# Gated linear attention in a one-core trunk: k's two parts stacked on the array's rows, v's two parts copied to the other half by DMA

## The chip, the cores and the metric

The kernel runs on one core of a Trainium2 chip. The metric is device time in microseconds (us) of one execution; the kernel before takes 2559.77 us, the median of 3 runs (2559.71 to 2559.84).

## What is computed

A trunk of two layers over 16 learned meta tokens and 1024 frames, width 1024. Layer 0 mixes with chunked gated linear attention (GLA), layer 1 with a sparse attention that the change doesn't touch; a SwiGLU follows each. Of the GLA, for each of 4 heads and each chunk of 64 positions:

```
cum = jnp.cumsum(gi, axis=2)
tot = cum[:, :, -1:, :]
S = jnp.exp(tot[:, :, 0, :, None]) * S + jnp.einsum(
    'bhcd,bhce->bhde', ki.astype(jnp.float32) * jnp.exp(tot - cum), vi.astype(jnp.float32))
o = jnp.einsum('bhcd,bhde->bhce', qi.astype(jnp.float32), S)
```

The state S of a head is 128 x 256 (key width by value width). A chunk adds k^T v to it, a product that contracts over 64 positions. Before it, S is scaled by the chunk's decay.

## The kernel before

Every fp32 operand of a product is split in two parts that TensorE takes in its fp32r type: a high part, which ScalarE casts, and a low part, which VectorE gets as the value less the high part (`split`, L224). A product is then the sum of three: high by high, high by low, low by high (`mm3`, L228).

The GLA stage goes through the four heads. For a head it projects q (in three stretches of tokens, L590), the output gate r (in six, L603), and then v, one tile of tokens at a time (`proj_tm`, L243): tile 0 holds the 16 meta tokens, tiles 1 to 8 hold 128 positions each, so two chunks: rows 0 to 63 and rows 64 to 127. After the projection of a tile, `core` (L513) splits v out of PSUM (`vh`, `vl`) and the decayed k out of SBUF (`kh`, `kl`), and puts three later steps on a list:

- `state` (L534), two ticks later: the products k^T v of the tile's two chunks, three each, into two PSUM tiles `us`; then VectorE adds them to the scaled state `sf` (L548), and the state is split into `sh` and `sl`.
- `read` (L554), four ticks later: q by the states of both chunks, 128 x 512 (L559), then the mean square on ScalarE (L564), its root, and the scaling on VectorE (L568).
- `gated` (L571), six ticks later: two transposes on TensorE (L575) and the gating on VectorE (L580).

`later.tick()` (L614) runs what is due after each tile, so on TensorE the order of a full tile's work is: projection of tile i, transposes of tile i-3, read of tile i-2, state of tile i-1, projection of tile i+1. A scheduler then sets the order within each of the other engines; each engine runs its own instructions in that order, and one that waits holds all behind it.

The two chunks of a tile lie on different rows of the array, and the six products alternate between them:

```
for step, (a, b) in enumerate([(kh, vh), (kh, vl), (kl, vh)]):
    for c, (r0, r1) in enumerate(halves):
        nc.tensor.matmul(us[c], a[r0:r1, :], b[r0:r1, :], start=step == 0, stop=step == 2)
```

GpSimd (POOL in the profile) issues few transfers in this stage, all of them from `rel_table` (L618), which head 1 calls for the layer after: four small writes of a bias table to DRAM (`s_rel`, L637), then eight transfers that write it out 128 times, shifted, per attention head (`s_skew`, L644, DRAM to DRAM). They go through the software DMA queue q0. Weights come by SyncE through q1.

Of the kernel before, what the change touches and what calls it, by code (L numbers as in the profile page):

```python
# [9 lines left out]
F32 = mybir.dt.float32  # L10
F32R = mybir.dt.float32r
# [99 lines left out]
class Trunk:  # L111
# [244 lines left out]
    def gla(self):  # L356
        nc, tc, io, w, later = self.nc, self.tc, self.io, self.w, self.later
        v = nc.vector
        with ExitStack() as ctx:
            g = ctx.enter_context(tc.tile_pool(name="gla", bufs=1))  # L360
            s2 = ctx.enter_context(tc.tile_pool(name="gla2", bufs=2))
            s3 = ctx.enter_context(tc.tile_pool(name="gla3", bufs=3))
            kt = g.tile([128, 9, 512], F32, name="kt")
# [124 lines left out]
            ats, step = {}, 0  # L488
# [3 lines left out]
            for tiles, j, i in order:  # L492
                if step in norms:
                    c, d = norms[step]
# [18 lines left out]
            def core(h, i, p, qh, ql, prev):  # L513
                rows = TT[i][1]
                two = i > 0
                hs = slice(h * 128, h * 128 + 128)
                vh = s3.tile([128, 256], F32R, name="vh")
                vl = s3.tile([128, 256], F32R, name="vl")
                kh = s3.tile([128, 128], F32R, name="kh")
                kl = s3.tile([128, 128], F32R, name="kl")  # L520
                if i == 0:
                    val = s3.tile([128, 256], F32, name="on")[:META, :]
                    self.meta(val, p[:, :256])
                else:
                    val = p[:, :256]
                self.split(vh[:rows, :], vl[:rows, :], val)
                self.split(kh[:rows, :], kl[:rows, :], kt[:rows, i, hs])
                st = {}
                sf = s2.tile([128, 512], F32, name="sf")
                sh = s2.tile([128, 512], F32R, name="sh")  # L530
# [1 line left out]
                cols = 512 if two else 256  # L532

                def state():  # L534
                    halves = [(0, 64), (64, 128)] if two else [(0, rows)]
                    us = [self.ps()[:, :256] for _ in halves]
                    for step, (a, b) in enumerate([(kh, vh), (kh, vl), (kl, vh)]):
                        for c, (r0, r1) in enumerate(halves):
                            nc.tensor.matmul(us[c], a[r0:r1, :], b[r0:r1, :], start=step == 0,
                                             stop=step == 2)  # L540
                    before = prev.get("s")
                    for c in range(len(halves)):
                        o = sf[:, c * 256 : c * 256 + 256]
                        uc = us[c]
                        if before is None:
                            v.tensor_copy(o, uc)
                        else:
                            v.scalar_tensor_tensor(o, before, dec[:, i, h, c : c + 1], uc,  # L548
                                                   op0=OP.mult, op1=OP.add)
                        before = o  # L550
                    prev["s"] = before
                    self.split(sh[:, :cols], sl[:, :cols], sf[:, :cols])
# [18 lines left out]
                def gated():  # L571
# [5 lines left out]
                    for j in range(2):  # L577
# [3 lines left out]
                                               self.gains[:, 5, k : k + 1], r, op0=OP.mult, op1=OP.mult)  # L581

                later.at(2, state)
                later.at(4, read)
                later.at(6, gated)
# [995 lines left out]
```

## Time and profile before

| | |
|---|---|
| median of 3 runs | 2559.77 us (2559.71 to 2559.84) |
| profiled execution, its own time | 2560.66 us |
| its span, first to last instruction | 2558.9 us |
| TensorE busy (PE) | 2506.4 us, 98% |
| VectorE (DVE), ScalarE (ACT), GpSimd (POOL) busy | 51%, 36%, 14% |
| mean granted clock of TensorE | 0.992 of full |
| products with k and v of `state` (L539) | 68 groups, from 142.2 to 405.0 us of the span |

The profile is one execution. Its rows give the start and the length of each instruction by engine, what it waited for, and for a DMA the time from issue to landing. A product's length in the rows holds its way through the array, so lengths of successive products overlap; what a product costs is the distance from its start to the next one's. "Granted clock" is the share of TensorE's full clock that the chip let through.

### The profile page before, as it was taken

Reading aid. Unit: us, or ns where it says so; the run is one execution under the profiler, and the core shown is the slowest. Engines: PE = TensorE matmul, PEld = TensorE weight load, DVE = VectorE, ACT = ScalarE, POOL = GpSimd, SP = SyncE. Lnnn points to the kernel's source line nnn. Section 1 sums busy time; section 2 is a strip of 40 time slices with the busy share of each in tenths; the row PEclk is TensorE's granted clock in tenths of the full one; section 3 lists DMA queues with packets and bytes.
Section 4 is the critical chain, followed back from the end, with each engine's and each line's share of the span. In section 5 each row is a group of like instructions: output and inputs, shape, how many; then the busy total and the mean of one; then the engine's idle time right before and its main releaser. Section 6 shows DMA issues by size and latency. Waiting matters only on the chain. (4 is left out here: it accounts for less than half of the span.)

```text
span 2558.9 us, 37579 instructions
## 1 busy us (share of the span) xinstructions
PE 2506.4 (98%) x15098; PEld 2325.8 (91%) x15098; DVE 1310.1 (51%) x2798; ACT 917.9 (36%) x1890; POOL 354.7 (14%) x461
## 2 busy tenths in 40 slices
PE   7999999999999999999999989999999999999997
PEld 6999999999999999999878979999988888888887
DVE  7575566643334433344769697753633333333336
ACT  5764453521111111111668567752511111111115
POOL 3000000111111111110202254521100000000001
PEclk9999999999999999999999999999999999999999
DMA  3113013123333333332321111131111111111111
GB/s 121 42 33 112 26 50 101 50 87 119 111 112 115 112 117 108 114 116 71 119 100 50 67 34 34 67 116 67 62 38 50 50 50 50 50 50 41 43 50 66
DMA packets 68786, 189.97 MB, mean 74 GB/s; under 512 B 7066, under 2 KB 18610, under 8 KB 65795
## 3 DMA queue, kind: packets, MB, share of 16 engines
q1 hardware_dynamic: 62642, 154.31, 18.0%
q0 software_dynamic: 5968, 33.26, 3.8%
q8 instruction: 118, 1.93, 0.3%
q14 instruction: 58, 0.47, 0.1%
HBM read 150.74 MB, written 41.58 MB: 75 GB/s over the span
## 5 line engine op out<-in xcount | busy, mean ns | idle before, releaser
L230 PE MATMUL ps<-xh,wh 128*128 128x344 f32 (+5 forms) x2808 | 946.9, 337 | 1.7 <-DVE qf L1039 1.3
L231 PE MATMUL ps<-xl,wh 128*128 128x344 f32 (+5 forms) x2808 | 943.0, 336 | 1.6 <-POOL xl L226 1.0
L232 PE MATMUL ps<-xh,wl 128*128 128x344 f32 (+5 forms) x2808 | 941.9, 335 | 1.9 <-DVE wl L197 1.9
L230 PEld LDWEIGHTS ps<-xh,wh 128*128 128x128 f32 x2808 | 529.2, 188 | 32.3 <-DVE qf L1039 1.6
L231 PEld LDWEIGHTS ps<-xl,wh 128*128 128x128 f32 x2808 | 529.6, 189 | 31.1 <-POOL xl L226 1.5
L232 PEld LDWEIGHTS ps<-xh,wl 128*128 128x128 f32 x2808 | 529.9, 189 | 29.0 <-DVE wl L197 2.5
L715 DVE TENSOR_TENSOR t<-sg,ps 128x344 f32<-128x344 f32 (+4 forms) x116 | 65.1, 561 | 639.3 <-PE ps L232 637.6
L192 ACT CAST wh<-wraw 128x1056 fp32r<-128x1056 f32 (+2 forms) x160 | 163.9, 1049 | 583.0 <-PE ps L231 576.2
L728 DVE TENSOR_TENSOR h<-h,ps 128x344 f32<-128x344 f32 (+3 forms) x456 | 251.4, 567 | 164.4 <-PE ps L232 164.3
L230 PE MATMUL ps<-hh,wh 128*128 128x512 f32 (+2 forms) x800 | 280.5, 351 | 0.0
L231 PE MATMUL ps<-hl,wh 128*128 128x512 f32 (+2 forms) x800 | 280.3, 350 | 0.0
L232 PE MATMUL ps<-hh,wl 128*128 128x512 f32 (+2 forms) x800 | 280.0, 350 | 0.0
L197 DVE TENSOR_TENSOR wl<-wraw,wh 128x1056 fp32r<-128x1056 f32 (+2 forms) x158 | 191.8, 1236 | 74.1 <-ACT wh L192 71.9
L230 PE MATMUL ps<-wh,xh 128*128 128x256 f32 (+9 forms) x560 | 171.9, 307 | 7.2 <-ACT xh L225 4.6
L232 PE MATMUL ps<-wh,xl 128*128 128x256 f32 (+9 forms) x560 | 167.3, 299 | 5.0 <-DVE xl L226 3.0
L714 ACT ACTIVATE sg<-ps 128x344 f32<-128x344 f32 (+4 forms) x116 | 57.7, 498 | 301.2 <-PE ps L232 301.1
L231 PE MATMUL ps<-wl,xh 128*128 128x256 f32 (+9 forms) x560 | 165.7, 296 | 0.0
L230 PEld LDWEIGHTS ps<-hh,wh 128*128 128x128 f32 x800 | 150.2, 188 | 14.6
L231 PEld LDWEIGHTS ps<-hl,wh 128*128 128x128 f32 x800 | 150.4, 188 | 14.3
L232 PEld LDWEIGHTS ps<-hh,wl 128*128 128x128 f32 x800 | 150.7, 188 | 13.8
L225 ACT CAST hh<-t 128x344 fp32r<-128x344 f32 (+4 forms) x116 | 60.1, 518 | 285.7 <-DVE t L715 285.7
L230 PEld LDWEIGHTS ps<-wh,xh 128*128 128x128 f32 x560 | 109.0, 195 | 13.2 <-ACT xh L225 4.9
(304 smaller groups left out, 3252.4 us busy)
## 6 DMA issues: line engine op xcount, KB each, us to landing
wraw<-in_w_fi SPq DMA_DIRECT2D x44, 528.0 KB, 3.9
wraw<-in_w_fi SPq DMA_DIRECT2D x44, 496.0 KB, 5.0
wraw<-in_w_fo SPq DMA_DIRECT2D x22, 528.0 KB, 3.9
wraw<-in_w_fo SPq DMA_DIRECT2D x22, 496.0 KB, 5.2
s_skew<-s_rel POOLq DMA_DIRECT2D x8, 583.5 KB, 14.2
h<-in_ht SPq DMA_DIRECT2D x8, 520.0 KB, 4.6
wraw<-s_skew SPq DMA_DIRECT2D x8, 520.0 KB, 3.5
sg<-in_w_dq SPq DMA_DIRECT2D x16, 256.0 KB, 4.2
```

The lines of the kernel that those rows point to most:

```text
L192: nc.scalar.copy(hi[:, a:e], r[:, : e - a])
L197: self.wlow.tensor_sub(lo[:, c:d], r[:, c - a : d - a], hi[:, c:d].bitcast(F32))
L225: self.nc.scalar.copy(hi, src)
L230: mm(p, sh, mh, start=first, stop=False, skip_group_check=True)
L231: mm(p, sh, ml, start=False, stop=False, skip_group_check=True)
L232: mm(p, sl, mh, start=False, stop=last, skip_group_check=True)
L714: nc.scalar.activation(sg[:, :n], pg[:, :n], AF.Silu)
L715: v.tensor_mul(t[:, :n], sg[:, :n], pu[:, :n])
L728: v.tensor_add(self.h[:, d, a : a + n], self.h[:, d, a : a + n], p[:, :n])
```

## The change

The three products of a chunk become two, over all 128 rows. `ks[:, c, :]` holds k's high part of chunk c on the chunk's own 64 rows and its low part on the other 64. `vs[:, c, :]` holds v's high part (columns 0 to 255) and low part (256 to 511) on both halves: they are computed on the chunk's own rows, and a transfer within SBUF, issued by GpSimd, copies them to the other rows. A product over 128 rows then sums (high k + low k) by high v, and a second one (high k + low k) by low v; low by low, left out before, is in it. The splits of v and k are made per chunk, so on 64 rows. Tile 0 keeps three products on its 16 rows. `ks` has three buffers, `vs` two.

```diff
-                vh = s3.tile([128, 256], F32R, name="vh")
-                vl = s3.tile([128, 256], F32R, name="vl")
-                kh = s3.tile([128, 128], F32R, name="kh")
-                kl = s3.tile([128, 128], F32R, name="kl")
+                ks = s3.tile([128, 2, 128], F32R, name="ks")
+                vs = s3.tile([128, 2, 512], F32R, name="vs", bufs=2)
...
-                self.split(vh[:rows, :], vl[:rows, :], val)
-                self.split(kh[:rows, :], kl[:rows, :], kt[:rows, i, hs])
+                if two:
+                    for c, (r, o) in enumerate(((0, 64), (64, 0))):
+                        own, src = vs[r : r + 64, c, :], slice(r, r + 64)
+                        self.split(own[:, :256], own[:, 256:], val[src, :])
+                        nc.gpsimd.dma_start(vs[o : o + 64, c, :], own)
+                        hi, ksrc = ks[r : r + 64, c, :], kt[src, i, hs]
+                        nc.scalar.copy(hi, ksrc)
+                        v.tensor_sub(ks[o : o + 64, c, :], ksrc, hi.bitcast(F32))
+                else:
+                    self.split(vs[:rows, 0, :256], vs[:rows, 0, 256:], val)
+                    self.split(ks[:rows, 0, :], ks[:rows, 1, :], kt[:rows, i, hs])
...
-                    halves = [(0, 64), (64, 128)] if two else [(0, rows)]
-                    us = [self.ps()[:, :256] for _ in halves]
-                    for step, (a, b) in enumerate([(kh, vh), (kh, vl), (kl, vh)]):
-                        for c, (r0, r1) in enumerate(halves):
-                            nc.tensor.matmul(us[c], a[r0:r1, :], b[r0:r1, :], start=step == 0,
-                                             stop=step == 2)
+                    us = [self.ps()[:, :256] for _ in range(2 if two else 1)]
+                    mm = nc.tensor.matmul
+                    for c, u in enumerate(us):
+                        if two:
+
+                            mm(u, ks[:, c, :], vs[:, c, :256], start=True, stop=False)
+                            mm(u, ks[:, c, :], vs[:, c, 256:], start=False, stop=True)
+                            continue
+                        mm(u, ks[:rows, 0, :], vs[:rows, 0, :256], start=True, stop=False)
+                        mm(u, ks[:rows, 0, :], vs[:rows, 0, 256:], start=False, stop=False)
+                        mm(u, ks[:rows, 1, :], vs[:rows, 0, :256], start=False, stop=True)
```

The instructions on TensorE, VectorE, ScalarE and GpSimd differ in the GLA stage alone; behind it the order is the same, but for line numbers (L539 becomes L549 and L550, L548 becomes L562, L564 becomes L578, L568 becomes L582, L580 becomes L594, L637 and L644 become L651 and L658).

TensorE, a full tile of head 0, from the end of `read` to the next projection. Before (`vh`, `vl`, `kh`, `kl` are the parts of v and k; x2 is one for each chunk):

```order
L231 MATMUL ps<-sl,qh 128x512
L232 MATMUL ps<-sh,ql 128x512
L539 MATMUL ps<-vh,kh 128x256 x2
L539 MATMUL ps<-vl,kh 128x256 x2
L539 MATMUL ps<-vh,kl 128x256 x2
L230 MATMUL ps<-wh,xh 128x256
```

And now:

```order
L231 MATMUL ps<-sl,qh 128x512
L232 MATMUL ps<-sh,ql 128x512
L549 MATMUL ps<-vs,ks 128x256
L550 MATMUL ps<-vs,ks 128x256
L549 MATMUL ps<-vs,ks 128x256
L550 MATMUL ps<-vs,ks 128x256
L230 MATMUL ps<-wh,xh 128x256
```

Six products on 64 rows became four on 128; their place between `read` and the next projection is the same.

ScalarE at the same place of head 0, now: the casts of v's two chunks in tile 5 (`vs_1633`), the squares of `read` (L578, `on_1657`) between them, with the engines that each waits for.

```order
L225 CAST vs_1633<-ps_1607 64x256 [waits DMASW5_49,DMASW6_49,PE_49,Activation_49]
L578 ACTIVATE on_1657,ss_1656<-ps_1652 64x256 [waits PE_49]
L578 ACTIVATE on_1657,ss_1656<-ps_1652 64x256
L225 CAST vs_1633<-ps_1607 64x256 [waits DVE_49]
L532 CAST ks_1778<-kt_92 64x128 [waits PE_49]
```

Before, one cast of 128 rows stood ahead of both squares; now the second chunk's cast stands behind them, and it waits for VectorE.

GpSimd around head 1, before: the small writes of the bias table, then the eight long ones, then the work of the next stage.

```order
L637 DMA s_rel<-rt_2288 8x396
L637 DMA s_rel<-rt_2293 8x396
L637 DMA s_rel<-rt_2298 8x264
L637 DMA s_rel<-rt_2339 8x111
L644 DMA s_skew<-s_rel 128x1167 x8
L226 TENSOR_TENSOR xl_68<-no_5341,xh_67 128x352
```

And now, with what each waits for (DMASW are the semaphores of transfers that GpSimd issued earlier; `vs_2339` is tile 1 of head 1, `vs_2391` tile 2, `vs_2449` tile 3):

```order
L651 DMA s_rel<-rt_2355 8x111 [waits Activation_49]
L530 DMA vs_2339<-vs_2339 64x512 [waits DMASW5_49,DMASW7_49,DMASW0_49,DVE_49]
L530 DMA vs_2339<-vs_2339 64x512 [waits DMASW6_49,DVE_49]
L658 DMA s_skew<-s_rel 128x1167 [waits DMASW3_49,DMASW4_49,DMASW2_49,DMASW1_49]
L530 DMA vs_2391<-vs_2391 64x512 [waits DVE_49] x2
L658 DMA s_skew<-s_rel 128x1167 x3
L658 DMA s_skew<-s_rel 128x1167 [waits DMASW5_49]
L658 DMA s_skew<-s_rel 128x1167 [waits DMASW6_49]
L658 DMA s_skew<-s_rel 128x1167 [waits DMASW7_49]
L658 DMA s_skew<-s_rel 128x1167 [waits DMASW0_49]
L530 DMA vs_2449<-vs_2449 64x512 [waits DMASW1_49,DVE_49]
L530 DMA vs_2449<-vs_2449 64x512 [waits DMASW2_49,DVE_49]
```

One `s_skew` transfer stands between the copies of tiles 1 and 2, and seven between those of tiles 2 and 3; behind them the copies of tiles 3 to 8 and of heads 2 and 3 follow on the same queue. Head 0 has its 16 copies ahead of `s_rel`.

## Rows read from the trace of the kernel before

**Rows 1.** The page: busy time, share of the span and instructions of each engine

```profile
PE 2506.4 (98%) x15098; PEld 2325.8 (91%) x15098; DVE 1310.1 (51%) x2798; ACT 917.9 (36%) x1890; POOL 354.7 (14%) x461
```

**Rows 2.** Busy time by stretch: stretch, length, PE, PEld, DVE, ACT, POOL, PEclk, DMA, GB/s

```profile
158.62:163.13 4.51, 4.51 (x37) 3.96 (x37) 4.12 (x16) 2.45 (x8) 0.00 (x0) 1.00 0.00 0
```

**Rows 3.** Timeline of TensorE, a tile of head 0: start, length (us), line, operation

```profile
157.53 0.38 PE L575 MATMUL ps<-ident,on 128*128 128x128 f32 x2
157.66 0.48 PE L230 MATMUL ps<-sh,qh 128*128 128x512 f32 x1
157.98 0.40 PE L231 MATMUL ps<-sl,qh 128*128 128x512 f32 x1
158.21 0.40 PE L232 MATMUL ps<-sh,ql 128*128 128x512 f32 x1
158.54 0.39 PE L539 MATMUL ps<-vh,kh 64*128 64x256 f32 x2
158.76 0.28 PE L539 MATMUL ps<-vl,kh 64*128 64x256 f32 x2
158.88 0.28 PE L539 MATMUL ps<-vh,kl 64*128 64x256 f32 x2
159.09 0.39 PE L230 MATMUL ps<-wh,xh 128*128 128x256 f32 x1
...
162.02 0.38 PE L575 MATMUL ps<-ident,on 128*128 128x128 f32 x2
```

**Rows 4.** Groups by line and shape, 139 to 410 us: busy us, mean ns

```profile
L226 DVE TENSOR_TENSOR vl<-ps,vh 128x256 fp32r<-128x256 f32 x32 | 13.5, 422 | 13.0 <-ACT vh L225 12.4
L225 ACT CAST vh<-ps 128x256 fp32r<-128x256 f32 x32 | 11.9, 372 | 26.6 <-PE ps L232 26.4
L226 DVE TENSOR_TENSOR kl<-kt,kh 128x128 fp32r<-128x128 f32 x30 | 8.6, 286 | 1.9 <-ACT kh L225 1.6 <-PE ps L232 0.2
```

**Rows 5.** Timeline of VectorE, head 0: small steps of the root, then with a split between

```profile
160.87 0.16 DVE L267 TENSOR_TENSOR rs<-rs 128x1 f32<-128x1 f32 x1
161.06 0.16 DVE L268 TENSOR_TENSOR rs<-rs 128x1 f32<-128x1 f32 x1
...
176.32 0.15 DVE L268 TENSOR_TENSOR rs<-rs 128x1 f32<-128x1 f32 x1
176.39 0.29 DVE L226 TENSOR_TENSOR kl<-kt,kh 128x128 fp32r<-128x128 f32 x1
```

**Rows 6.** DMA issues: transfer, queue, count, KB each, us from issue to landing

```profile
wraw<-in_onehot SPq DMA_DIRECT2D x1, 132.0 KB, 2.3
s_rel<-rt POOLq DMA_DIRECT2D x1, 3.5 KB, 2.8
wh<-s_dq_h POOLq DMA_DIRECT2D x4, 1024.0 KB, 5.2
```

**Rows 7.** Timeline of ScalarE, head 0: tile 1, and the tile of rows 3

```profile
143.31 0.41 ACT L225 CAST sh<-sf 128x256 fp32r<-128x256 f32 x1 [0.28 <-DVE sf L546]
...
159.52 0.20 ACT L564 ACTIVATION_READ_ACCUMULATOR on<-ps 64x1 f32 x1
```

**Rows 8.** Timeline of TensorE, head 0: tile 1's first state product

```profile
145.78 0.39 PE L539 MATMUL ps<-vh,kh 64*128 64x256 f32 x2
```

**Rows 9.** Timeline of GpSimd, head 1: the eight long transfers' issues

```profile
222.34 4.10 POOL L644 DMA_DIRECT2D s_skew<-s_rel  x8 [2.79 <-DMA s_rel<-rt]
```

**Rows 10.** `s_skew` alone: from issue to landing, the first transfer, then the eighth

```profile
DMA to landing us min/median/max: 7.6/7.6/7.6
...
DMA to landing us min/median/max: 17.5/17.5/17.5
```

**Rows 11.** Busy time by stretch: the long transfers (DMA share, GB/s at the end)

```profile
224.00:242.00 18.00, 18.00 (x145) 16.11 (x144) 14.93 (x54) 10.62 (x32) 2.44 (x5) 1.00 0.95 260
```

**Rows 12.** Timeline of TensorE, head 1: tile 3's first state product

```profile
229.79 0.39 PE L539 MATMUL ps<-vh,kh 64*128 64x256 f32 x2
```

**Rows 13.** Busy time by stretch: TensorE at a lower granted clock

```profile
68.00:74.00 6.00, 5.84 (x23) 4.82 (x24) 6.00 (x11) 3.78 (x11) 2.91 (x3) 0.51 0.00 0
```

More of the change, by code (lines that the diff above doesn't have):

```diff
@@ L534, in state @@
                 def state():
-                    halves = [(0, 64), (64, 128)] if two else [(0, rows)]
-                    us = [self.ps()[:, :256] for _ in halves]
-                    for step, (a, b) in enumerate([(kh, vh), (kh, vl), (kl, vh)]):
-                        for c, (r0, r1) in enumerate(halves):
-                            nc.tensor.matmul(us[c], a[r0:r1, :], b[r0:r1, :], start=step == 0,
-                                             stop=step == 2)
+                    us = [self.ps()[:, :256] for _ in range(2 if two else 1)]
[8 more added lines that the diff above has]
+                        mm(u, ks[:rows, 1, :], vs[:rows, 0, :256], start=False, stop=True)
                     before = prev.get("s")
-                    for c in range(len(halves)):
+                    for c in range(len(us)):
                         o = sf[:, c * 256 : c * 256 + 256]
```

## The prediction

> **What bounds the kernel now.** I read the page's busy shares first: TensorE is busy 98% of the span [rows 1], so what is saved on it is saved in the end, and what makes it wait is lost. Then the stretch of one tile of head 0, because an average over the kernel says nothing about this stage: there TensorE has no gap, VectorE is busy 4.12 of 4.51 us [rows 2]. So the stage has one full engine and one nearly full. Then TensorE's timeline of that tile [rows 3]: from one pair of transposes (157.53) to the next (162.02) is 4.49 us, the price of a tile.
>
> **The products.** In rows 3 the six products stand as three pairs, each pair with one start: the two chunks run side by side on their halves of the array. The price is read from distances between starts. A 256-column product in a row of its kind costs 0.12 (158.76 to 158.88). The last read product, 512 columns, costs 0.23 when its like follows (157.98 to 158.21) but 0.33 before the pairs; the first pair costs 0.22 and the last 0.21. So the group costs 0.10 ahead of it + 0.22 + 0.12 + 0.21 = 0.65 us: three slots of 0.12 and about 0.1 of extra at each change of shape. The change puts four products of the common shape there: 4 x 0.12 = 0.48. It saves 0.17 us a tile, 32 tiles, **5.4 us**, and nothing else on TensorE. The tile costs 4.32. The Trainium skill, TensorEngine Tiling (Array Packing), Tiling Modes, speaks against the change: tiles of 64 rows work independently and in parallel. By that alone three slots become four, and the sum would be 32 x 0.12 = 3.8 us slower; the same section says that a change of mode drains the array, and the three extra gaps in rows 3 agree with it.
>
> **The splits.** Each split of v and k is now made twice on half the rows. The length goes by columns, so I take the same price for 64 rows: per tile VectorE gets 0.42 + 0.29 more, ScalarE 0.37 and a cast of k, no longer [rows 4]. ScalarE has room (2.45 of 4.51 [rows 2]). VectorE has not; but in its new order the small steps of the root alternate with the splits of k and the update of the state, where before they stood in a chain. In a chain such a step comes 0.19 us after the last; ahead of a split that doesn't need it it costs 0.07 [rows 5], and of some five such places each gives 0.12 back. I take 0.1 us of the 0.71 as left, VectorE's tile at about 4.6 us beside the 4.49 of now, hidden by the waits below, and price the rest as a rival.
>
> **The wait for v's copy.** This is new: `state` now waits for a chain of casts, subtractions, GpSimd's issue and a transfer. The trace has no transfer within SBUF. The nearest rows for the time from issue to landing: 2.3 us for 132 KB issued by SyncE, 2.8 for a small one by GpSimd, 5.2 for 1 MB by GpSimd [rows 6]. The copy has 128 KB; I take **2.8**, the row of its own queue, and keep 2.3 and 3.3 for the range (5.2 is eight times the bytes).
> - *A full tile, head 0.* I count from the end of its projection (157.53). The second chunk's cast stands behind the squares of `read`, which end at 159.72 [rows 7], so at +2.2; cast 0.37, subtraction 0.42 and handing over put the issue at +3.15 and the landing at +5.95. TensorE wants it one tile (4.32) and transposes, read and the first chunk's products (0.13 + 0.78 + 0.24) later, at +5.47. It waits 0.48. That delay gives the next tile's copy as much room, so about every other wait falls away: 0.24 a tile, for tiles 3 to 7 together 1.2 us. Queued behind TensorE's wait is everything it does; behind GpSimd's only further copies.
> - *Tile 1 of a head.* There is no read yet, so TensorE comes early: 145.78 [rows 8], and 0.24 later for the second chunk. The second cast stands behind that of `sh`, which ends at 143.72 [rows 7]; with 0.37, 0.42 and handing over behind a subtraction of `sl`, the issue comes at 144.75 and the landing at 147.55. Wanted at 146.0: a wait of 1.5.
> So a head waits 2.7 us; heads 0, 2 and 3 **8.1 us**.
>
> **The long transfers in head 1.** This is the term that decides. GpSimd issues eight `s_skew` transfers from 222.34 to 226.44, 0.51 each [rows 9]. The first landed 7.6 us after its issue, at 229.9; the eighth, issued at 225.9, after 17.5, at 243.4; six others between in the order of issue [rows 10]. From 224 to 242 the 16 DMA engines were 95% busy at 260 GB/s [rows 11]. In the new order all eight stand ahead of the copies of tile 3 on GpSimd, seven of them behind tile 2's, in the same DMA queue, and the copies wait in addition for semaphores that the earlier transfers use. If the queue is served in order, tile 3's copy lands when the eighth has landed: 243.4, plus 1.0 for the two copies of tile 2 that now lie between (256 KB at 260 GB/s), plus about 0.5 of its own, so at about 245. TensorE's products of that tile started at 229.79 [rows 12] and can't be passed. That is **15.2 us** of delay up to there, with the waits of tiles 1 and 2 of this head and the two tiles' saving in it. For tiles 4 to 7 I add 1.0. TensorE stands idle for some 10 us of it (and some 4 at tile 2, whose copy stands behind the first long transfer). Where it idled before, the granted clock fell: from 68 to 74 us it was 0.51, the lower of the two levels, 1.2 GHz [rows 13], which costs half of 6 us. I take **2 us**, between 0 (it falls and rises within the idle time) and 3.5.
>
> **The sum.** -5.4 + 0.3 (two tiles' saving, counted in the 15.2) + 8.1 + 15.2 + 1.0 + 2.0 = +21.2 us. The profiled execution took 2560.66 with a span of 2558.9; the median of 3 is 0.9 below it, and the difference counts on either. Forecast: 2559.8 + 21.2 = **2581 us**. Its own range: a copy that lands after 2.3 or 3.3 us shifts every later wait by up to 0.25 a tile and tile 1's by 0.5, about 1.5 us a head, -6 or +6 in all; the clock -2 or +1.5: 2573 to 2589.
>
> **The rivals.**
> 1. *The copies pass the long transfers.* If the queue shares its engines among transfers, tile 3's copy needs only to be issued: the first long transfer landed at 229.9 [rows 10], and the second chunk's copy waits for a semaphore that the second one uses, free some 2.5 us later; it lands near 235.5. Head 1 loses about 5.5 in place of 15.2, and no clock: -5.1 + 8.1 + 5.5 + 1.0 = +9.5, 2569 us. For it: the first long one took 7.6 us, more than an eighth of the 21 that all took. Against: they landed one by one in order of issue.
> 2. *VectorE becomes the bound.* If the alternation hides nothing, a full tile needs 4.49 + 0.71 = 5.2 us on VectorE, 0.88 above TensorE's 4.32; five tiles of four heads give 17.6 in place of 4.6 us of waits there (3 x 1.2 + 1.0), 13 more: 2594 us. For it: how full VectorE is [rows 2]; against: [rows 5]. It decides from about 4.6 us a tile on.
> 3. *GpSimd's issue is held up.* If an issue had to wait for VectorE's instruction to end, up to the longest of its stage, some 0.7 us, each copy lands that much later: at most 0.35 a tile and 0.7 for tile 1, so 8 to 9 us over four heads, 2590 us. Against: the eight issues took 4.10 us, 0.51 each, and VectorE was busy 14.93 of 18 us there [rows 9, 11]. The Trainium skill, SBUF — State Buffer, SBUF: two separate sides, has the rule: a DMA from GpSimd can't have its descriptors written while VectorE runs in certain two-port modes; those 0.51 us show no such stall.
> 4. *Not slower: the copies land in time.* If a copy lands within about 2.0 us and those of head 1 are let through at once, only tile 1's wait stays, some 0.7 a head, and the saving stays: -5.4 + 2.8 = -2.6, 2557 us; with no waits at all 2554.4. It decides at a landing of 2.3 us for the full tiles (5.95 less 5.47 below 2.8), and for head 1 at a queue that lets small transfers by. Against: 2.8 for the small one of GpSimd [rows 6].
> 5. *The count of products.* By the lengths of 0.28 in rows 3, one product fewer in each of 64 chunks would save 18 us; the pairs with one start exclude it.
>
> **How the numbers follow.** Forecast 0.62, copies pass 0.18, VectorE 0.09, held-up issue 0.05, not slower 0.05, others 0.01. A change of 0.2% is 5.1 us, about what a measurement of this kernel can tell from none. Below 2554.7 lies only the end of the fourth rival: faster 0.03. Within 0.2% lie the rest of it and the low end of the first: same 0.06. Slower 0.91. The range takes in the forecast's own 2573 to 2589, nearly all of the first rival (2569, 4 either way), the third and the lower part of the second: 2565 to 2592.
>
> **What would show it.** Right: in head 1 a gap of about 10 us on TensorE ahead of tile 3's state products, ended by the DMA of `vs`, with the landing of the last `s_skew` just before it; a lower clock for some us after it; in heads 0, 2 and 3 a gap of 1 to 2 us ahead of tile 1's and some of 0.3 to 0.8 later; products of 0.12 us, four to a tile. Wrong: a small gap in head 1 (rival 1), VectorE without idle time and TensorE waiting for `sl` or for PSUM (rival 2), issues of the copies longer than 0.5 us (rival 3), no gaps at all (rival 4).

## The result and the profile after

The changed kernel takes 2587.84 us, the median of 4 runs (2587.49 to 2588.48); the kernel before, in the same session, 2559.81 (2559.71 to 2560.50). The ratio is 1.0109, with an interval of 1.0097 to 1.0120: 28.0 us slower. The forecast was 2581 us with a range of 2565 to 2592, so the sign and the range hold, and the time lies 6.8 us above the forecast.

Two lines of the page of the changed kernel, the busy times and one of the DMA issues (transfer, queue, count, KB each, median us from issue to landing):

```profile
PE 2508.5 (97%) x15034; PEld 2332.1 (90%) x15034; DVE 1336.7 (52%) x2862; ACT 939.6 (36%) x1954; POOL 387.5 (15%) x525
...
vs<-vs POOLq DMA_DIRECT2D x64, 128.0 KB, 2.2
```

Against [rows 1] TensorE's busy time hardly moved while the span grew by 26.8 us (2585.7 in place of 2558.9): the loss is idle time. And the copy within SBUF, which no row of before could price, lands after 2.2 us in the median, a little under the forecast's 2.8.

TensorE's timeline of the changed kernel, in head 0 (start and length in us; in brackets the idle time before and what ended it):

```profile
146.84 0.36 PE L549 MATMUL ps<-vs,ks 128*128 128x256 f32 x1 [0.67 <-DMA vs<-vs]
...
154.95 0.35 PE L549 MATMUL ps<-vs,ks 128*128 128x256 f32 x1 [0.16 <-DMA vs<-vs]
...
159.00 0.28 PE L549 MATMUL ps<-vs,ks 128*128 128x256 f32 x1
159.11 0.28 PE L550 MATMUL ps<-vs,ks 128*128 128x256 f32 x1
159.23 0.28 PE L549 MATMUL ps<-vs,ks 128*128 128x256 f32 x1
159.35 0.28 PE L550 MATMUL ps<-vs,ks 128*128 128x256 f32 x1
159.47 0.28 PE L230 MATMUL ps<-wh,xh 128*128 128x256 f32 x1
...
164.51 0.35 PE L549 MATMUL ps<-vs,ks 128*128 128x256 f32 x1 [0.74 <-DMA vs<-vs]
...
169.36 0.36 PE L549 MATMUL ps<-vs,ks 128*128 128x256 f32 x1 [0.39 <-DVE rs L270]
```

Four products cost 0.47 us (159.00 to 159.47), and without a wait they are as good as the forecast had them [rows 3]. But each head has a handful of waits for v's copies, most of them for the second chunk's. A releaser like `rs` at the end is the latest event by the profile; the product itself needs `vs` and `ks`.

The same timeline in head 1, at tile 3:

```profile
246.45 0.55 PE L549 MATMUL ps<-vs,ks 128*128 128x256 f32 x1 [12.06 <-DMA vs<-vs]
246.80 0.41 PE L550 MATMUL ps<-vs,ks 128*128 128x256 f32 x1
```

The products that ran at 229.79 before [rows 12] now run at 246.45, behind 12.06 us of idle time. Why so late is told by the transfers' own rows, which answer to [rows 9, 10]: the last two `s_skew`, then a copy of tile 3 and the last one issued behind it (issue, and time to landing):

```profile
L658 POOL DMA_DIRECT2D s_skew<-s_rel x2: 515/515/515, 230.0 to 230.5; - x2
DMA to landing us min/median/max: 15.0/15.3/15.5
...
L530 POOL DMA_DIRECT2D vs<-vs x1: 541/541/541, 231.0 to 231.0; - x1
DMA to landing us min/median/max: 15.3/15.3/15.3
...
L530 POOL DMA_DIRECT2D vs<-vs x1: 509/509/509, 239.5 to 239.5; - x1
DMA to landing us min/median/max: 7.8/7.8/7.8
```

The eighth `s_skew` lands at about 246.0 (230.5 + 15.5), the copy issued behind it at 246.3, one issued at 239.5 at 247.3. They land one by one in the order of their issue.

Busy time by stretch of the changed kernel (columns as in [rows 2]): the idle time, the 4.6 us behind it, the next 5, and three tiles of head 0:

```profile
240.00:244.00 4.00, 0.00 (x0) 0.00 (x0) 0.00 (x0) 0.00 (x0) 0.00 (x0) 0.50 1.06 323
246.40:251.00 4.60, 4.55 (x21) 4.58 (x22) 2.23 (x5) 1.21 (x3) 0.00 (x0) 0.50 0.01 2
251.00:256.00 5.00, 5.00 (x41) 4.86 (x40) 2.93 (x10) 3.03 (x10) 1.02 (x2) 0.98 0.18 37
...
162.30:176.70 14.40, 12.32 (x85) 10.87 (x84) 13.62 (x46) 9.09 (x26) 2.93 (x6) 1.00 0.30 61
```

After the idle time TensorE ran 4.6 us at a granted clock of 0.50, the lower level, with 21 products where 41 go into the next 5 us: about 2 us lost. And in the three tiles of head 0 VectorE is busy 13.62 of 14.40 us, more than TensorE, and between 157 and 176 us it has no gap above 0.04 us: a sign that a second thing is wrong in this stage.

It shows in VectorE's own timeline: the starts of one and the same instruction of four successive tiles, the scaling by the root.

```profile
159.26 0.98 DVE L582 TENSOR_SCALAR on<-ps,rs 64x256 f32<-64x256 f32 x2
...
164.38 0.98 DVE L582 TENSOR_SCALAR on<-ps,rs 64x256 f32<-64x256 f32 x2
...
169.26 0.98 DVE L582 TENSOR_SCALAR on<-ps,rs 64x256 f32<-64x256 f32 x2
...
174.62 0.97 DVE L582 TENSOR_SCALAR on<-ps,rs 64x256 f32<-64x256 f32 x2
```

(174.62 - 159.26) / 3 = 5.12 us a tile, where TensorE's work, in a tile without a wait, is 4.24 and the forecast had 4.6 for VectorE.

The copies go out later for it. In the tile whose projection ends at 158.08 the first chunk's cast on ScalarE is done at 158.70, and VectorE comes to the subtraction 1.57 us later, behind steps of the root and the scaling of another tile:

```profile
158.33 0.37 ACT L225 CAST vs<-ps 64x256 fp32r<-64x256 f32 x1 [0.34 <-PE ps L232]
...
160.27 0.42 DVE L226 TENSOR_TENSOR vs<-ps,vs 64x256 fp32r<-64x256 f32 x1
```

The second chunk's cast waits for that subtraction, and its copy is issued at 162.17.

To see which head pays, the table gives for each kernel below the time from the first state product of a head's tile 0 to that of the next head, and for head 3 to its last state product, all read from TensorE's timeline of the profiled execution. Among head 3's last state products TensorE already does products of the next stage, at 0.16 us each, and not equally many: 48 stand ahead of the last state product before, 51 in the change, 58 in the change without copies, 64 with all remedies. So this column counts work that is no loss. The column behind it runs on to the first product that reads `hh`, in the next stage, by which every kernel has done the same work there; it is the one to compare. The last column is the median of the runs. Medians of the kernel before in these sessions lay between 2559.78 and 2560.63, its single runs between 2557.8 and 2561.2, so differences of 1 us between rows of that column mean nothing.

| kernel | head 0 | head 1 | head 2 | head 3, last state | head 3 to `hh` | median, us |
|---|---|---|---|---|---|---|
| before | 75.76 | 73.44 | 73.38 | 40.32 | 200.40 | 2559.8 |
| the change | 78.82 | 90.80 | 76.49 | 44.44 | 203.78 | 2587.8 |
| copies by SyncE | 78.05 | 87.59 | 76.47 | 44.01 | 203.35 | 2583.7 |
| change without copies | 75.12 | 72.81 | 72.81 | 43.12 | 201.47 | 2561.7 |
| before, split by halves | 75.73 | 73.44 | 73.39 | 44.01 | 203.33 | 2563.5 |
| products alone | 73.63 | 71.26 | 71.24 | 38.89 | 198.84 | 2552.0 |
| early table | 79.21 | 76.38 | 76.48 | 44.55 | 203.89 | 2574.1 |
| early table, k low on GpSimd | 78.40 | 75.58 | 75.52 | 46.01 | 204.99 | 2572.2 |
| the same, state later | 79.57 | 74.63 | 74.64 | 43.21 | 202.95 | 2570.2 |
| no copies, k low on GpSimd | 73.67 | 73.16 | 71.39 | 42.77 | 200.95 | 2556.6 |
| early table, casts first | 79.66 | 76.33 | 76.33 | 45.00 | 204.22 | 2572.4 |
| all remedies | 74.10 | 72.16 | 72.15 | 44.93 | 202.94 | 2559.5 |
| all remedies in heads 0 to 2 | 74.52 | 71.52 | 71.35 | 40.30 | 200.36 | 2554.9 |
| before, early table | 76.17 | 73.46 | 73.39 | 40.47 | 200.44 | 2560.7 |

The four heads with the column to `hh` make 422.98 us before and 449.89 in the change: of the 28.0 us by the medians the profiled executions show 26.9 in this stage.

### The profile page after: what moved, and what is told of

It is laid out like the page before. It is cut to its first block, busy times and chain, and to the rows that moved or that the text cites. A ratio compares the mean times of both kernels' runs of the same rounds, so it can differ in the third digit from the quotient of the medians.

```text
span 2585.7 us, 37811 instructions
## 1 busy us (share of the span) xinstructions
PE 2508.5 (97%) x15034; PEld 2332.1 (90%) x15034; DVE 1336.7 (52%) x2862; ACT 939.6 (36%) x1954; POOL 387.5 (15%) x525
## 5 line engine op out<-in xcount | busy, mean ns | idle before, releaser
L231 PEld LDWEIGHTS ps<-hl,wh 128*128 128x128 f32 x800 | 150.3, 188 | 14.3
L232 PEld LDWEIGHTS ps<-hh,wl 128*128 128x128 f32 x800 | 150.5, 188 | 13.9
```

Of the source, the lines that this page charges most:

```text
L231: mm(p, sh, ml, start=False, stop=False, skip_group_check=True)
L232: mm(p, sl, mh, start=False, stop=last, skip_group_check=True)
```

## The experiments

**1. Copies by SyncE.** Is it the queue that makes head 1's copies late, or the full DMA engines?

```
-                        nc.gpsimd.dma_start(vs[o : o + 64, c, :], own)
+                        nc.sync.dma_start(vs[o : o + 64, c, :].bitcast(F32), own.bitcast(F32))
```

> The change with v's copies issued by SyncE on its own queue in place of GpSimd's. Theory (the copies of tile 3 of head 1 stand in order behind the eight s_skew transfers in one queue): they now pass, the idle time of 12.06 us ahead of tile 3's state products goes, and head 1 costs what head 0 and head 2 cost (3.1 us in place of 17.4): 2587.8 - 14.3 = 2573.5 us. Rival (the copies are late because the 16 DMA engines are full, whatever the queue): head 1 keeps most of its loss, 2584 or more.

Measured: 2583.67 us, 4.2 less than the change, where 14.3 were expected; the rival had 2584 or more. The queue's theory as stated falls. TensorE's timeline in head 1 at the second chunks of tile 2 and of tile 3, and at tile 3's first between them:

```profile
235.46 0.55 PE L549 MATMUL ps<-vs,ks 128*128 128x256 f32 x1 [6.78 <-DMA vs<-vs]
...
241.18 0.28 PE L549 MATMUL ps<-vs,ks 128*128 128x256 f32 x1
...
244.42 0.36 PE L549 MATMUL ps<-vs,ks 128*128 128x256 f32 x1 [2.85 <-DMA vs<-vs]
```

The issues of tile 2's two copies (the one landing on record is that of the second), then of tile 3's first copy, and the last of the eight `s_skew` transfers:

```profile
L530 SPq DMA_DIRECT2D vs<-vs x2: 461/462/462, 223.8 to 225.9; - x2
DMA to landing us min/median/max: 9.4/9.4/9.4
...
L530 SPq DMA_DIRECT2D vs<-vs x1: 461/461/461, 229.0 to 229.0; - x1
DMA to landing us min/median/max: 7.4/7.4/7.4
...
L658 POOL DMA_DIRECT2D s_skew<-s_rel x1: 517/517/517, 228.6 to 228.6; - x1
DMA to landing us min/median/max: 16.5/16.5/16.5
```

And the stretch of the first wait:

```profile
229.00:235.00 6.00, 0.00 (x0) 0.00 (x0) 0.44 (x2) 0.00 (x0) 0.11 (x1) 0.82 1.03 297
```

Copies do pass long transfers now: tile 3's first, issued at 229.0 behind all eight, lands at 236.4, and the eighth lands at 245.1. Tile 3's products run at 241.18 and 244.42 in place of 246.45. But beside transfers that fill the engines (share 1.03, 297 GB/s) a copy takes up to 9.4 us in place of 2.2. That one is tile 2's second, which held nothing up for so long in the change (230.36 there, 235.46 here); tile 3 waits anew for its own, and head 1 ends only 3.2 us sooner. A load of weights ahead of them in SyncE's queue isn't the reason: the last one was issued at 219.4 and had landed at 223.7. So both are true: in one queue the order decides, and another queue gets a copy through no faster than the shared engines let it.

**2. The change without copies.** What is left when nothing waits for a transfer?

```
-                        nc.gpsimd.dma_start(vs[o : o + 64, c, :], own)
...
-                vs = s3.tile([128, 2, 512], F32R, name="vs", bufs=2)
+                vs = vss[(h * 9 + i) % 2]
```

> The change without the transfer within SBUF: v's parts lie in two fixed buffers whose other halves hold zeros, so the output lacks the low part of k times v; products, splits and their order of dependence on VectorE and ScalarE stay. Theory 1 (what is left of the loss outside head 1 is the wait for the copy): no waits, only the saving of 0.25 us a tile that the tile of 4.24 us in the changed trace shows: 2559.8 - 8 = 2552 us. Theory 2 (VectorE, whose full tile takes 5.1 us in the changed trace, bounds tiles 5 to 8): tile 1's waits go, 1.2 us a head, but some 2 us a head stay, which eat the saving: 2560, 2558 to 2563.

Measured: 2561.70 us, 1.8 above before, ratio 1.0007 (0.9997 to 1.0016), so not told apart from it; the stage itself takes 422.21 us in the profile, 0.8 less than before. Theory 2: the saving of the products is eaten by something that isn't the copy. VectorE's scaling in head 0, as above, and TensorE behind head 3, at the first products of the next stage:

```profile
157.74 0.97 DVE L588 TENSOR_SCALAR on<-ps,rs 64x256 f32<-64x256 f32 x2
...
162.72 0.97 DVE L588 TENSOR_SCALAR on<-ps,rs 64x256 f32<-64x256 f32 x2
...
167.61 0.97 DVE L588 TENSOR_SCALAR on<-ps,rs 64x256 f32<-64x256 f32 x2
```

```profile
395.09 0.58 PE L230 MATMUL ps<-xh,wh 128*128 128x344 f32 x2 [0.94 <-DVE h L600]
```

VectorE takes 4.9 us a tile, TensorE 4.22 up to tile 6 (starts of the state products 157.06, 161.28, 165.50). VectorE has no gap above 0.04 us from 157 to 176 us, so the 4.9 are its own work. Each tile leaves it some 0.7 us further behind. In heads 0 to 2 the distance between the steps takes up most of that, and the projections of the next head's q and r give VectorE time to catch up; against the products alone a head loses 1.5 us, at tiles 7 and 8 and behind them. Behind head 3 the next stage needs `h` at once, and there the arrears cost 2.6 us (201.47 less 198.84).

**3. The kernel before, split by halves.**

```
-                self.split(vh[:rows, :], vl[:rows, :], val)
-                self.split(kh[:rows, :], kl[:rows, :], kt[:rows, i, hs])
+                for r0, r1 in [(0, 64), (64, 128)] if two else [(0, rows)]:
+                    self.split(vh[r0:r1, :], vl[r0:r1, :], val[r0:r1, :])
+                    self.split(kh[r0:r1, :], kl[r0:r1, :], kt[r0:r1, i, hs])
```

> The kernel before, with its six products, but v and k split per 64-row half as in the change; nothing else. Theory 2 (VectorE bounds): a full tile of VectorE grows from 4.49 to about 5.1 us, 0.6 over TensorE's 4.49; after a slack of about a tile's wait, three to four tiles a head pay it, some 2 us a head: 2568, 2564 to 2572. Theory 1 (the splits hide in VectorE's alternation, as the prediction had it): 2560, 2559 to 2562.

Measured: 2563.47 us, 3.5 above before, ratio 1.0013 (1.0004 to 1.0023): between the ranges of the two theories. The heads tell why: heads 0, 1 and 2 take what they took (75.73, 73.44, 73.39), and all of it stands behind head 3 (203.33 in place of 200.40). At TensorE's old pace of 4.49 us a tile the splits do hide; only the arrears at the end are paid.

**4. The products alone.** Four products over all rows, with the full-height splits of before:

```
...
+                            nc.tensor.matmul(us[c], (kh, kl)[c], vh, start=True, stop=False)
+                            nc.tensor.matmul(us[c], (kh, kl)[c], vl, start=False, stop=True)
...
```

> The kernel before, with its full-height splits, but four products over 128 rows in place of six over 64 (k's high part for the first chunk, its low part for the second, by v's two parts, over all rows; so the output is another sum). Prices the products alone. By the prediction 0.17 us a tile: 2554.4 us. By the changed trace, where an undelayed tile takes 4.24 in place of 4.49 us: 2551.8 us. If VectorE's 4.49 us a tile already bounds before: 2558 to 2560.

Measured: 2551.97 us, 7.9 less than before, ratio 0.9969 (0.9957 to 0.9980): the saving is 0.25 us a tile, not 0.17. TensorE's timeline of this kernel around one group:

```profile
157.62 0.28 PE L539 MATMUL ps<-vh,kh 128*128 128x256 f32 x1
157.73 0.28 PE L540 MATMUL ps<-vl,kh 128*128 128x256 f32 x1
...
158.09 0.28 PE L230 MATMUL ps<-wh,xh 128*128 128x256 f32 x1
158.21 0.28 PE L231 MATMUL ps<-wl,xh 128*128 128x256 f32 x1
...
161.85 0.28 PE L539 MATMUL ps<-vh,kh 128*128 128x256 f32 x1
```

The projection's first product costs 0.12 here (158.09 to 158.21). In the kernel before it starts at 159.09 [rows 3], and the next one follows at

```profile
159.31 0.28 PE L231 MATMUL ps<-wl,xh 128*128 128x256 f32 x1
```

so it cost 0.22: a fourth place of extra time, behind the last pair, that the forecast's sum of three had left out. A tile takes 4.23 us here (157.62 to 161.85), and VectorE with full-height splits keeps up with it: no product of heads 0 to 2 waits for anything above 0.1 us.

**5. Early table.** Head 1's long transfers moved to where nothing waits for GpSimd:

```
+                if h == 1:
+                    self.rel_table(s2)
                 wq = w.get("gq%d" % h)
...
-                if h == 1:
-                    self.rel_table(s2)
```

> The change with the bias table for the layer after (its products, small writes and the eight s_skew transfers) called ahead of head 1's q in place of ahead of its v, so that the long transfers are over before v's copies begin; all else as in the change. Theory (all that head 1 loses over the other heads, 14.3 us, its lower clock with it, comes of the long transfers, part by the order in the queue, part by the full engines): 2587.8 - 14.3 = 2573.5 us, 2572 to 2576, and no wait of TensorE for vs above 1.5 us. Rival (something else in head 1 costs, or the loss moves to the weights' loads, which now meet the long transfers): above 2578.

Measured: 2574.11 us (2572.05 to 2574.85), 13.7 less than the change; no wait for `vs` in head 0 is above 0.75 us, and head 1 takes 76.38 us, as head 2 does (76.48). The theory holds: the long transfers, with the lower clock behind them, are worth 13.7 us, and nothing else in head 1 is special.

**6. A control.** The same move in the kernel before.

> A control: the kernel before with the bias table called ahead of head 1's q, nothing else. Theory (in the kernel before nothing in this stage waits for GpSimd's queue, so the place of the long transfers costs nothing, and the 13.7 us that the early table gave back to the change are the change's own): 2559 to 2561. Rival (the early table is worth something by itself): 2557 or less.

Measured: 2560.69 us, ratio 1.0004 (0.9995 to 1.0013). The place of the long transfers is worth nothing where nobody waits for their queue; experiment 5 measured the change, not the table.

**7. k's low part on GpSimd, without copies.**

```
-                        v.tensor_sub(ks[o : o + 64, c, :], ksrc, hi.bitcast(F32))
+                        nc.gpsimd.tensor_sub(ks[o : o + 64, c, :], ksrc, hi.bitcast(F32))
```

> The run without copies (2561.7 us; its other halves hold zeros, so the low part of k times v is left out), and k's low part on GpSimd. Theory (VectorE is what costs 9.7 us over the run of the products alone, 2552.0): some two thirds go, 2555, 2553 to 2558. Rival (it is ScalarE's doubled casts or the order, not VectorE's load): 2560 to 2562.

Measured: 2556.58 us, ratio 0.9987 (0.9977 to 0.9996): 5.1 of the 9.7 us between experiments 2 and 4 are gone (by the stage 3.0 of 7.2), with 0.58 us a tile moved from VectorE to GpSimd and nothing else. It is VectorE's load that costs there. The rest stands behind head 3 (200.95 against 198.84) and in head 1 (73.16 against 71.26), where GpSimd issues the eight long transfers (219.11 to 223.24) ahead of its next subtractions; that this is the reason, no run shows.

**8. k's low part on GpSimd, with copies and the early table.** The same edit.

> The run with the early bias table, and the subtractions of k's low part (two a tile, 0.29 us each on VectorE) done by GpSimd. Theory (VectorE's full tile of 5.1 us, over TensorE's 4.2, is what holds tiles 5 to 8 and the end of head 3 and makes the copies' issues late): VectorE's tile falls to about 4.5, and most of the 9.7 us between the two runs without the copy goes: 2566, 2563 to 2569. Rival (only the transfer's own 2.2 us count): 2572 to 2574.

Measured: 2572.20 us (2570.88 to 2574.20), the rival. Against experiment 5 heads 0 to 2 gain 0.8 to 1.0 us each. GpSimd's timeline shows what came in the way of more:

```profile
161.19 0.51 POOL L530 DMA_DIRECT2D vs<-vs  x1 [2.67 <-DVE h L594]
162.19 0.45 POOL L533 TENSOR_TENSOR ks<-kt,ks 64x128 fp32r<-64x128 f32 x1 [0.50 <-ACT ks L532]
162.60 0.55 POOL L530 DMA_DIRECT2D vs<-vs  x1
```

GpSimd now does the first chunk's subtraction, which waits for ScalarE's cast, ahead of the second chunk's issue, at 162.60. 2.3 us later the copy is there, and TensorE waits 0.22 us for it (164.97). Part of what VectorE gave back, the engine that issues the copy took; how much, no run separates. And head 3 loses 1.1 us (204.99 against 203.89): behind two waits of 0.66 and 1.22 us for copies of `vs` the granted clock stood at its lower level there, where experiment 5 has 1.00 in the same part of the head.

```profile
402.70:405.20 2.50, 2.50 (x14) 2.50 (x13) 1.78 (x7) 2.10 (x6) 0.51 (x1) 0.50 0.68 115
```

**9. The state later.** Half a projection (1.4 us) more for the copy, on top of experiment 8:

```
         for k in range(KT):
+            if k == KT // 2 and mid:
+                mid()
...
-                later.at(2, state)
+                if 1 <= i <= 6:
+                    mids[i + 2] = state
+                else:
+                    later.at(2, state)
```

> The run before this one, and the state products of tiles 1 to 6 put half a projection later (behind the first half of the projection of the tile two on), so 1.4 us later on TensorE. Theory (a copy that is in time costs nothing): the waits for vs go, and the products' saving of 8 us is left but for VectorE's rest: 2556, 2552 to 2560, so faster than the kernel before. Rival (what is left is VectorE, and the shorter time from state to read turns the wait into one for sh and sl): 2563 or more.

Measured: 2570.20 us (2568.28 to 2570.32), far above the theory and in the rival's range; but the waits in heads 1 and 2 all stand at state products, and none at the read that the rival named. Yet tiles 1 to 5 of head 0 show no wait at all, with 4.24 us a tile. The loss moved to tile 7, whose state stands at the old place and so comes 1.4 us sooner behind the others:

```profile
172.36 0.36 PE L553 MATMUL ps<-vs,ks 128*128 128x256 f32 x1 [1.34 <-DMA vs<-vs]
173.48 0.55 PE L553 MATMUL ps<-vs,ks 128*128 128x256 f32 x1 [0.65 <-ACT on L582]
```

In head 0 these waits cost more than their length: the granted clock stood at its lower level behind them.

```profile
173.60:176.60 3.00, 3.00 (x10) 2.98 (x11) 2.82 (x12) 1.42 (x4) 1.40 (x3) 0.50 0.22 44
```

Three us at half the clock are about 1.5 lost, so head 0 takes longer than in experiment 8 (79.57 for 78.40), while heads 1 and 2, at a clock of 1.00, gain 0.9 each.

**10. Casts first.** In the change ScalarE sat idle ahead of the second chunk's cast until VectorE's subtraction of the first (0.45 us ahead of the cast at 160.72). Written one behind the other, on top of experiment 5:

```
+                    for c, r in enumerate((0, 64)):
+                        nc.scalar.copy(vs[r : r + 64, c, :256], val[r : r + 64, :])
...
-                        self.split(own[:, :256], own[:, 256:], val[src, :])
+                        v.tensor_sub(own[:, 256:], val[src, :], own[:, :256].bitcast(F32))
```

> The run with the early bias table, and one edit: ScalarE's two casts of v's high part are written one behind the other, ahead of VectorE's two subtractions, so that the second cast no longer waits for the first subtraction. Theory (the waits of the heads are for the second chunk's copy, whose chain of cast, wait, cast, subtraction, issue and 2.2 us of transfer ends late): the second copy comes some 0.5 us sooner wherever VectorE isn't behind, tile 1's second wait (0.68 us) and tile 3's (0.15) go, some 0.8 us a head and about as much later on: 2574.1 - 5 = 2569 us, 2567 to 2572. Rival (VectorE, full, decides when the second copy starts, in whatever order the casts stand): 2573 to 2575.

Measured: 2572.37 us (2572.04 to 2574.97), between the two and within the scatter of experiment 5: not settled by the time. In the trace the two casts run as one piece,

```profile
162.81 0.76 ACT L528 CAST vs<-ps 64x256 fp32r<-64x256 f32 x2
```

and tile 1's second wait in head 0 falls from 0.68 to 0.37 us, while heads 1 and 2 take what they took (76.33 each). So the order of the casts shows no gain in these heads.

**11. All remedies.** Experiments 5 and 7 to 10, copies by SyncE, tile 7's steps a tick later, and one half of the scaling moved to ScalarE:

```
...
+                        if c == 0:
+                            nc.scalar.mul(on[r0:r1, :], o[r0:r1, :256], y[r0:r1, :])
...
```

> All remedies together: early bias table, copies issued by SyncE, casts of v ahead of the subtractions, k's low part on GpSimd, the first chunk's scaling by the root on ScalarE, the state products half a projection later (tile 7's one tick later, with its read and gating). Theory (with the long transfers gone, the copy in time and VectorE's tile down to about 4.1 us, only the products' saving of 8.0 us is left): 2553 us, 2551 to 2557, faster than the kernel before (2559.8). Rival (the later state only moves the wait to the read that needs sh and sl, or the waits of SyncE hold up the loads of weights): 2560 or more.

Measured: 2559.53 us beside 2560.63 of before, ratio 0.9997 (0.9987 to 1.0006): no difference. Heads 0 to 2 take 218.41 us where before takes 222.58, and head 3 gives 2.5 of these 4.2 us back (202.94 in place of 200.40); the rest of the 44.93 at its last state product is work of the next stage done sooner. At its end TensorE waits for VectorE:

```profile
394.53 0.40 PE L230 MATMUL ps<-xh,wh 128*128 128x344 f32 x1 [1.01 <-DVE on L591]
...
413.07 0.44 PE L598 MATMUL ps<-ident,on 128*128 128x128 f32 x2 [0.91 <-DVE on L591]
```

**12. All remedies in heads 0 to 2.** Head 3 with the products, splits and order of the kernel before:

```
...
+                new = two and h < 3
...
```

> The run with all remedies in heads 0 to 2, and in head 3 the products, splits and order of the kernel before. Theory (the remedies hold in heads 0 to 2, which ran 4.2 us shorter than before, 218.4 in place of 222.6 us, and the loss stands at the end of head 3 alone, where VectorE's arrears meet the next stage: 44.9 in place of 40.3 us): 2560 - 4.2 = 2556 us, 2554 to 2557.5, faster than the kernel before by more than its runs scatter. Rival (the loss at the end comes from elsewhere, and moves): 2559 to 2561.

Measured: 2554.89 us, the median of 11 runs, beside 2559.78, ratio 0.9981 (0.9972 to 0.9990). It is faster than both kernels: 4.9 us less than before, 33 less than the change as made. So head 3 in its new form is most of what kept experiment 11 from gaining (2.6 of 3.6 us by the table, with the column to `hh`); its products, splits and order went back together, and which of them it is, no run separates.

## Why the prediction was right, and where it was off

By differences of medians the 28.0 us are made up so: products -7.9 (experiment 4), splits +9.7 (2 less 4), copies without long transfers +12.4 (5 less 2), long transfers +13.7 (the change less 5). By the stage alone, from the table (heads 0 to 2 and head 3 to `hh`), the same differences are -8.0, +7.2, +13.8 and +13.9, in sum 26.9. The two ways part at the change without copies, whose median lies 2.6 us higher against before than its stage does; the cause of that lies outside the stage and is open. So splits and copies are known to some 2 us each.

- **The products.** Forecast -5.4, measured -7.9. The mechanism was right: three slots of pairs and extra time at each change of shape. The term was mis-sized because the sum of 0.65 us stopped at the projection's start; its first product cost 0.22 too. 0.75 less 0.48 is 0.27 a tile. The rule of the Trainium skill, TensorEngine Tiling (Array Packing), Tiling Modes, that tiles of 64 rows work in parallel would have made this part 3.8 us slower; the pairs do run in parallel, and the runs show the part 7.9 us faster all the same, since the four places of extra time in a tile, some 0.1 us each, cost more than the fourth slot.
- **The splits.** This is the step that failed: "I take 0.1 us of the 0.71 as left, VectorE's tile at about 4.6 us beside the 4.49 of now, hidden by the waits below". VectorE's tile takes 5.12 us in the changed kernel and 4.9 without copies, in both without a gap. With full-height splits it kept up with 4.23 (experiment 4), so the 4.49 from which the forecast counted was TensorE's pace and not VectorE's need, and nearly all of the 0.71 came on top: alternating the small steps with the splits gave back next to nothing. The sum had the term at nothing; it cost 7.2 to 9.7 us, beside 3.5 at TensorE's old pace (experiment 3). Rival 2 was near the size of the tile (5.2), and its sign of a VectorE without idle time came; but TensorE waits for `vs`, and the price was wrong in kind: TensorE doesn't pay VectorE's excess tile by tile. The arrears are taken up by the distance between the steps and by the next head's projections, and what is not is paid at tiles 7 and 8 of a head and behind head 3 (experiments 2, 3 and 11).
- **The wait for v's copy.** Forecast 2.7 us a head; measured 12.4 to 13.8 over four heads, 3.1 to 3.4 a head. The landing (2.2 in place of 2.8) was better than taken, the issue later, because VectorE was behind: the second chunk's copy goes out 4.1 us behind the end of its projection (158.08 to 162.17, above), where the forecast had 3.15. Tile 1 of head 0 waited 0.47 and 0.67 us where 1.5 was forecast, and the full tiles more than the 1.2. The point from which rival 4 was to decide, a landing within 2.3 us, was met, and the waits stayed.
- **The long transfers.** Right in mechanism and size. Forecast: the copy of tile 3 lands at about 245, TensorE idles some 10 us, 2 us more for the clock, and some 4 at tile 2. Measured: 246.3 (in a head that starts 2.4 us later, at 220.39 in place of 217.96), 12.06 us, about 2, and 0.86 at tile 2, whose first copy landed at 229.9, right behind the first long transfer, which itself took 4.8 us in place of 7.6. Against before head 1 lost 17.4 us; the forecast's terms for it (15.2, 1.0, 2.0, less six tiles' saving of 0.17) make 17.2. Rival 1 had copies that pass lose head 1 only 5.5 us; in experiment 1 they do pass, on another queue, and head 1 still loses 14.2 (87.59 less 73.44).
- **The held-up issue**, rival 3: not seen. The 64 issues took 0.51 us in the median and at most 0.61, and in the full tiles VectorE was busy 13.62 of 14.40 us. So no stall of the kind that the Trainium skill tells of in SBUF — State Buffer, SBUF: two separate sides, appears in this kernel.

So 5.7 of the error of 6.8 us lie in this stage, and nearly all of them in heads 0, 2 and 3, which lost 3.1, 3.1 and 3.4 us against before (head 3 to `hh`), where the forecast had 1.3 each (2.7 of waits less eight tiles' saving): the products are 1.7 better there, the splits 5.7 worse (experiment 2 less 4 in these heads) and the copies 1.6 worse (the change less experiment 2: 9.7 in place of 8.1). Left open is how the 21 to 22 us of splits and copies divide where both are late at once: each of experiments 2, 7, 8 and 9 takes away one and meets the other.

That the time falls in the forecast's own 2573 to 2589 is in part luck. That range allowed for the copy's landing and for the clock. The landing came out below it, which by the forecast's own count takes up to 6 us off; the splits, which it held for hidden, and the later issues put more than that back. The sign, and what happened in head 1, were forecast for the reason that the runs show.

## What to carry to other kernels

Before a transfer is put on a queue, read what else is issued there and when: two copies of 128 KB behind eight long transfers cost more than all the products saved, and moving the long ones cost nothing. An engine that falls behind by a constant each tile shows no wait for a long time; look for its bill where the next consumer has no slack, in a head's last tiles and behind the stage. And where an operation's price goes by its columns, doing it in two halves of its rows doubles it: 0.71 us a tile on an engine that was 91% busy took back nearly all of the 0.25 saved on the bound one, or more (7.2 to 9.7 of 8 us).

## What the runs showed of the hardware that was not expected

- A copy of 128 KB within SBUF lands 2.2 us after its issue, from GpSimd's queue and from SyncE's alike (medians over a kernel's 64 issues); beside transfers that fill the DMA engines the SyncE ones took up to 9.4 us.
- Going back from products on 64 rows to 128 rows costs extra on the first product of the new shape too (0.22 for 0.12), so a group of pairs amid full-height products costs about 0.4 us more than its slots.
- A subtraction of 64 x 128 elements takes 0.45 us on GpSimd and 0.29 on VectorE, no less than the 0.29 of 128 x 128 [rows 4].
